# Residual-trunk kernel: in the down projections, one DMA-made sum is made by VectorE, and two operand sums are asked for later

## The chip, the cores and the metric

The kernel runs on 1 core of one Trainium2 chip. The time is the device time of one execution in microseconds (us); of several executions the median is taken. The engines are named as in the profile: PE (TensorE matmul), PEld (its weight loads), DVE (VectorE), ACT (ScalarE), POOL (GpSimd), SP (SyncE, which issues plain loads).

## What is computed

Two layers of a decoder trunk over 512 tokens of 1024 features, in float32. Each layer has four sub-layers: a SwiGLU feed-forward network, a token mixer, a cross-attention to 256 memory tokens, and a second SwiGLU network. The change lies in the feed-forward networks alone, of which there are four (two per layer):

```python
def swiglu_ffn(h, w_gu, w_down):      # w_gu (1024, 5632), w_down (2816, 1024)
    gu = h @ w_gu
    gate, up = jnp.split(gu, 2, axis=-1)
    return (jax.nn.silu(gate) * up) @ w_down

for i in range(DEPTH):                # DEPTH = 2
    f = swiglu_ffn(rms_norm(h, ffn1_pre_g[i]), ffn1_w_gu[i], ffn1_w_down[i])
    h = h + 0.5 * rms_norm(f, ffn1_post_g[i])
    ...                               # mixer and cross-attention
    f = swiglu_ffn(rms_norm(h, ffn2_pre_g[i]), ffn2_w_gu[i], ffn2_w_down[i])
    h = h + 0.5 * rms_norm(f, ffn2_post_g[i])
```

## The kernel before

**Split numbers.** Every float32 matrix is split into a high part (`whi` for weights, the first half of a `big` tile for operands), a cast by ACT (line 74), and a low part (`wlo`, or the second half of `big`), a subtraction by DVE (line 75). A product of two such numbers is three matmuls: lines 79 (high by high), 80 (high by weight low), 81 (operand low by weight high).

**The feed-forward network.** The 2816 hidden features are worked through in three groups, `FF_PARTS`. In each group the gate and up projections come first (`fm_quad`, then `seven` once per pair of 128 features, on the raw weights of line 242), then the down projection of that group. The first two groups hold 1024 features each, and their down projection is `seven_tm`, which is called eight times in the program: four times for a first group (here *first part*; its results are copied into the sums) and four times for a second group (*second part*; its results are added to them). The third group has a routine of its own.

**`seven_tm`** multiplies a 2 by 2 block matrix of hidden values (r11, r12, r21, r22) with a 2 by 2 block matrix of weights in seven block products in place of eight. The factors are sums of blocks: on the operand side x1 = r21 - r22, x2, x3 = r11 - r21 (line 414) and x4 (line 417), all by DVE; on the weight side T1 and T3. A block of weights is two tiles `raw`, called halves here, of 128 by 1024 numbers (512 KB) each. The products run on PE in this order: b11, T1 with x1, T1 (plus b22) with x2, b21 with r12, **T3 with x3**, b22 with x4, T1 (now with b21) with r22. Each product is 24 matmuls, 12 for each half of its weights.

**Sums of weights.** `load` (line 347) brings a block from HBM through SP; `put` (line 352) sends a second block from HBM onto the same tile with the DMA's own adder (`accum_op`), issued by POOL, which waits for the plain load to land first. T3 is block (0, 1) by `load` plus block (1, 1) by `put`. Block (1, 1) lies in the kernel's memory too, as b22, since its own product needs it. DVE already adds b22 to T1 (line 404).

**What sets the order.** The instructions of each engine run in a fixed order which a scheduler of the language lays down when the program is built; it starts from the order of the code and moves an instruction ahead of another where its model has it ready sooner. Each engine waits at the head of its own list for semaphores. Buffers limit how far ahead an engine may run: seven `raw` tiles, four `whi` and four `wlo` tiles. A `raw` tile is free for the next load once DVE has made its low part; a `whi` tile is free once PE has done the last of its 12 matmuls.

**Names.** The tiles carry numbers in the order of the built program. In the first call, `raw_1290` and `raw_1292` are the two halves of T3, `raw_1162` and `raw_1164` those of b22, `raw_1152` and `raw_1154` those of T1, `raw_1166` and `raw_1168` those of b21; in the second call (a second part) the same are `raw_2490`, `raw_2492`; `raw_2364`, `raw_2366`; `raw_2354`, `raw_2356`; `raw_2368`, `raw_2370`. Lines 387, 389 and 391 (in `take`) bring a product's result out of PSUM.

Of the kernel before, what the change touches and what calls it, by code (L numbers as in the profile page):

```python
# [8 lines left out]
ALU = mybir.AluOpType  # L9
# [26 lines left out]
def trunk_kernel(tc, x, mem, ffn1_pre_g, ffn1_w_gu, ffn1_w_down, ffn1_post_g,  # L36
# [7 lines left out]
    nc = tc.nc  # L44
    with ExitStack() as es:
# [290 lines left out]
        def seven_tm(w, k0, r, a11, f, fresh):  # L336
# [13 lines left out]
            def put(raws, kh, ch):  # L350
                for kk in range(2):
                    nc.gpsimd.dma_start(out=raws[kk], in_=rows(kh, kk, ch), accum_op=ALU.add)  # L352
# [16 lines left out]
            def product(n, raws, ops):  # L369
                start = n not in banks  # L370
                if start:
                    banks[n] = [psa(), psa()]
                for kk in range(2):
                    wh = parts(raws[kk], (P, 2, 512))
                    for s_ in range(2):
                        for i in range(2):
                            k = 2 * kk + i
                            cs = slice(s_ * P, (s_ + 1) * P)
                            mm3(banks[n][s_], (ops[:, 0, k, cs], ops[:, 1, k, cs]), (wh[0][:, i], wh[1][:, i]),
                                start and k == 0, k == 3, False)  # L380
                return banks[n]

            def take(th, ch, ps, how):
                for s_ in range(2):
                    dst = f[th][:, s_, ch * 512:(ch + 1) * 512]
                    if how is None:
                        nc.scalar.copy(out=dst, in_=ps[s_])
                    elif how == "from":
                        nc.vector.tensor_tensor(out=dst, in0=ps[s_], in1=dst, op=sub)
                    else:  # L390
                        nc.vector.tensor_tensor(out=dst, in0=dst, in1=ps[s_], op=how)
# [16 lines left out]
            a12 = operand(r12)  # L408
            u2 = product("A", t1, x2)
            t3 = load(0, 1)  # L410
            put(t3, 1, 1)
            put(t1, 1, 0)
            take(0, 1, u2, None if fresh else "from")
            nc.vector.tensor_tensor(out=r11, in0=r11, in1=r21, op=sub)
            x3 = operand(r11)
            take(0, 0, product("B", b21, a12), add)
            nc.vector.tensor_tensor(out=e, in0=e, in1=r12, op=add)
            x4 = operand(e)
            take(1, 1, product("A", t3, x3), sub)
            a22 = operand(r22)  # L420
            take(0, 1, product("C", b22, x4), "from")
            take(1, 0, product("A", t1, a22), None if fresh else add)
# [552 lines left out]
        rows = qt([P, P])  # L975
# [64 lines left out]
```

## Time and profile before

| | us |
|---|---|
| median of 3 runs | 2033.12 (2029.88 to 2033.5) |
| the profiled execution, its own time | 2035.78 |
| its span, first to last instruction | 2034.1 |
| PE busy in the span | 1962.7 (96%) |
| DVE busy | 1488.5 (73%) |
| ACT busy | 1037.4 (51%) |
| mean granted clock of PE, share of full speed | 0.993 |

The span is 1.7 us shorter than the execution's own time. "Busy" is the time in which an engine has at least one instruction running; the matmuls of PE overlap one another and their ends are modelled, so two matmuls in a row that show no idle time between them can still start late. Where an exact figure is wanted, the starts of matmuls are compared. "DMA share" is the mean busy share of the core's 16 DMA engines.

### The profile page before, as it was taken

How to read it: one execution, taken by the hardware profiler on the slowest of the kernel's cores; microseconds unless marked ns; L12 is line 12 of the kernel's file. 1: busy time of each engine (PE TensorE's matmuls, PEld its weight loads, DVE VectorE, ACT ScalarE, POOL GpSimd, SP SyncE). 2: the span in 40 equal slices, each digit the busy share in tenths (PEclk: the TensorE clock that was granted, in tenths of full speed). 3: DMA queues.
4: the chain of work that ended last, by engine and by line, in shares of the span. 5: the costliest groups of instructions: out<-in, count | busy, mean ns of one | idle time of the engine just before them, and what ended most of it. 6: DMA issues, size and time to landing. Idle time of an engine off the chain costs nothing. (4 is left out here: it accounts for less than half of the span.)

```text
span 2034.1 us, 31756 instructions
## 1 busy us (share of the span) xinstructions
PE 1962.7 (96%) x12841; PEld 1788.2 (88%) x12841; DVE 1488.5 (73%) x1831; ACT 1037.4 (51%) x1477; POOL 234.0 (12%) x229
## 2 busy tenths in 40 slices
PE   7999999998999999999999999999999999999998
PEld 7979889888878879899898979989878879989797
DVE  6776877799956558777886877787666648776875
ACT  6555445543555355555454555445535545545452
POOL 1111110122011011110101111110000001111100
PEclk9999999999999999999999999999999999999999
DMA  6877685323642145787873668696152225787771
GB/s 198 217 166 198 161 212 155 110 89 124 225 148 94 52 114 139 172 202 181 191 214 73 169 156 204 169 215 197 53 186 73 83 52 145 184 200 198 172 189 44
DMA packets 245929, 311.51 MB, mean 153 GB/s; under 512 B 9500, under 2 KB 189300, under 8 KB 244758
## 3 DMA queue, kind: packets, MB, share of 16 engines
q1 hardware_dynamic: 189158, 233.93, 35.9%
q0 software_dynamic: 56448, 75.51, 21.9%
q8 instruction: 100, 1.64, 0.3%
q14 instruction: 47, 0.39, 0.1%
q10 hardware_dynamic: 176, 0.05, 0.0%
HBM read 303.15 MB, written 6.29 MB: 152 GB/s over the span
## 5 line engine op out<-in xcount | busy, mean ns | idle before, releaser
L79 PE MATMUL psa<-big,whi 128*128 128x256 f32 (+1 forms) x3056 | 885.2, 291 | 6.2 <-ACT big L74 4.5
L81 PE MATMUL psa<-big,wlo 128*128 128x256 f32 (+1 forms) x3056 | 885.4, 290 | 5.6 <-DVE wlo L75 5.6
L80 PE MATMUL psa<-big,whi 128*128 128x256 f32 (+1 forms) x3056 | 887.1, 291 | 0.8 <-DVE big L75 0.8
L74 ACT CAST whi<-raw 128x1024 fp32r<-128x1024 f32 x522 | 544.3, 1049 | 622.8 <-PE psa L80 275.4
L75 DVE TENSOR_TENSOR wlo<-raw,whi 128x1024 fp32r<-128x1024 f32 x522 | 635.6, 1225 | 283.1 <-ACT whi L74 280.6
L79 PEld LDWEIGHTS psa<-big,whi 128*128 128x128 f32 x3056 | 587.6, 193 | 16.7 <-ACT big L74 8.3
L81 PEld LDWEIGHTS psa<-big,wlo 128*128 128x128 f32 x3056 | 588.0, 193 | 13.6 <-DVE wlo L75 6.7
L80 PEld LDWEIGHTS psa<-big,whi 128*128 128x128 f32 x3056 | 588.7, 193 | 9.1 <-DVE big L75 1.8
L79 PE MATMUL psa<-whi,big 128*128 128x512 f32 x864 | 341.5, 397 | 19.2 <-ACT whi L74 11.5
L80 PE MATMUL psa<-wlo,big 128*128 128x512 f32 x864 | 340.4, 394 | 6.1 <-DVE wlo L75 6.1
L81 PE MATMUL psa<-whi,big 128*128 128x512 f32 x864 | 339.3, 395 | 0.5
L79 PEld LDWEIGHTS psa<-whi,big 128*128 128x128 f32 x864 | 162.9, 189 | 60.7 <-ACT whi L74 16.6
L80 PEld LDWEIGHTS psa<-wlo,big 128*128 128x128 f32 x864 | 164.0, 190 | 42.7 <-DVE wlo L75 9.7
L81 PEld LDWEIGHTS psa<-whi,big 128*128 128x128 f32 x864 | 163.8, 190 | 39.7 <-DVE big L75 5.8
L302 POOL DMA_DIRECT2D raw<-in_ffn_w_gu_dram x40 | 51.6, 1289 | 611.9 <-DMA raw<-in_ffn_w_gu_dram 419.2
L158 POOL TENSOR_TENSOR r<-m,nhalf 128x1 f32<-128x1 f32 x74 | 49.0, 662 | 461.0 <-DVE m L532 182.3
L352 POOL DMA_DIRECT2D raw<-in_ffn_w_down_dram x48 | 57.3, 1193 | 332.7 <-DMA raw<-in_ffn_w_down_dram 229.5
L729 DVE SCALAR_TENSOR_TENSOR big<-big,par 128x511 f32<-128x511 f32 (+29 forms) x120 | 85.7, 767 | 0.0
L79 PE MATMUL psa<-big 128*128 128x512 f32 (+1 forms) x224 | 80.9, 363 | 0.8 <-ACT big L74 0.8
L297 POOL DMA_DIRECT2D raw<-in_ffn_w_gu_dram x40 | 53.0, 1326 | 244.7 <-DMA raw<-in_ffn_w_gu_dram 223.4
L80 PE MATMUL psa<-big 128*128 128x512 f32 (+1 forms) x224 | 80.7, 360 | 0.0
L81 PE MATMUL psa<-big 128*128 128x512 f32 (+1 forms) x224 | 80.2, 359 | 0.0
(150 smaller groups left out, 1658.2 us busy)
## 6 DMA issues: line engine op xcount, KB each, us to landing
raw<-in_ffn_w_gu_dram SPq DMA_DIRECT2D x216, 512.0 KB, 4.8
raw<-in_ffn_w_down_dram SPq DMA_DIRECT2D x104, 512.0 KB, 4.0
raw<-in_ffn_w_gu_dram POOLq DMA_DIRECT2D x80, 512.0 KB, 7.8
raw<-in_ffn_w_down_dram POOLq DMA_DIRECT2D x48, 512.0 KB, 6.1
raw<-in_xa_w_kv_dram SPq DMA_DIRECT2D x32, 512.0 KB, 3.5
raw<-in_ev_w_in_dram SPq DMA_DIRECT2D x16, 512.0 KB, 4.3
raw<-in_xa_w_q_dram SPq DMA_DIRECT2D x16, 512.0 KB, 3.7
raw<-in_xa_w_o_dram SPq DMA_DIRECT2D x16, 512.0 KB, 3.9
```

Of the source, the lines that this page charges most:

```text
L74: nc.scalar.copy(out=hi, in_=src)
L75: nc.vector.tensor_tensor(out=lo, in0=src, in1=hi.bitcast(F32), op=ALU.subtract)
L79: nc.tensor.matmul(out=ps, lhsT=lhs[0], rhs=rhs[0], start=start, stop=skip, skip_group_check=skip)
L80: nc.tensor.matmul(out=ps, lhsT=lhs[0], rhs=rhs[1], start=False, stop=skip, skip_group_check=skip)
L81: nc.tensor.matmul(out=ps, lhsT=lhs[1], rhs=rhs[0], start=False, stop=stop or skip, skip_group_check=skip)
L158: nc.gpsimd.tensor_tensor(out=r, in0=m, in1=nhalf.broadcast_to([P, n]), op=ALU.pow)
L297: nc.gpsimd.dma_start(out=t1, in_=fm_rows(w, 0, ca), accum_op=ALU.add)
L302: nc.gpsimd.dma_start(out=t3, in_=fm_rows(w, 1, cb), accum_op=ALU.add)
L352: nc.gpsimd.dma_start(out=raws[kk], in_=rows(kh, kk, ch), accum_op=ALU.add)
L729: nc.vector.scalar_tensor_tensor(out=acc[:, c, s_:], in0=z[:, c, :SEQ - s_], scalar=par[:, c, CONV - 1 - s_:CONV - s_], in1=acc[:, c, s_:] ...
```

## The change

Only `seven_tm` is changed. The second half of T3 is no longer completed by the DMA's adder: its `put` is dropped, and DVE adds the second half of b22 to it (new line 417). The first half stays with the DMA's adder (new line 411). In the code the product of b21 now stands ahead of the sum for x3, and the product of T3 ahead of the sum for x4. Behind the new line the line numbers are one or two higher (the sum for x3 is line 415, that for x4 line 419).

```diff
--- before.py
+++ after.py
@@ -408,15 +408,16 @@
             a12 = operand(r12)
             u2 = product("A", t1, x2)
             t3 = load(0, 1)
-            put(t3, 1, 1)
+            nc.gpsimd.dma_start(out=t3[0], in_=rows(1, 0, 1), accum_op=ALU.add)
             put(t1, 1, 0)
             take(0, 1, u2, None if fresh else "from")
+            take(0, 0, product("B", b21, a12), add)
             nc.vector.tensor_tensor(out=r11, in0=r11, in1=r21, op=sub)
             x3 = operand(r11)
-            take(0, 0, product("B", b21, a12), add)
+            nc.vector.tensor_tensor(out=t3[1], in0=t3[1], in1=b22[1], op=add)
+            take(1, 1, product("A", t3, x3), sub)
             nc.vector.tensor_tensor(out=e, in0=e, in1=r12, op=add)
             x4 = operand(e)
-            take(1, 1, product("A", t3, x3), sub)
             a22 = operand(r22)
             take(0, 1, product("C", b22, x4), "from")
             take(1, 0, product("A", t1, a22), None if fresh else add)
```

DVE, first call, a first part: from the sum for x4 (line 417 before, 419 after) on. `wlo_1345` and `wlo_1361` are the low parts of T3's halves before, `wlo_1341` and `wlo_1357` after; `big_1301` and `big_1336` are x3. Before:

```order
L417 TENSOR_TENSOR q4_1170<-q4_1170,big_220 128x1024
L75 TENSOR_TENSOR big_1255<-big_220,big_1255 128x1024
L75 TENSOR_TENSOR wlo_1323<-raw_1168,whi_1322 128x1024
L75 TENSOR_TENSOR wlo_1345<-raw_1290,whi_1344 128x1024
L75 TENSOR_TENSOR big_1301<-big_219,big_1301 128x1024
L75 TENSOR_TENSOR wlo_1361<-raw_1292,whi_1360 128x1024
L391 TENSOR_TENSOR big_1209<-big_1209,psa_1304 128x512
L75 TENSOR_TENSOR big_1341<-q4_1170,big_1341 128x1024
L391 TENSOR_TENSOR big_1209<-big_1209,psa_1305 128x512
```

After:

```order
L419 TENSOR_TENSOR q4_1170<-q4_1170,big_220 128x1024
L75 TENSOR_TENSOR big_1255<-big_220,big_1255 128x1024
L75 TENSOR_TENSOR wlo_1318<-raw_1168,whi_1317 128x1024
L75 TENSOR_TENSOR wlo_1341<-raw_1290,whi_1340 128x1024
L417 TENSOR_TENSOR raw_1292<-raw_1292,raw_1164 128x1024
L75 TENSOR_TENSOR big_1336<-big_219,big_1336 128x1024
L75 TENSOR_TENSOR wlo_1357<-raw_1292,whi_1356 128x1024
L75 TENSOR_TENSOR wlo_1382<-raw_1162,whi_1381 128x1024
L391 TENSOR_TENSOR big_1209<-big_1209,psa_1299 128x512
L391 TENSOR_TENSOR big_1209<-big_1209,psa_1300 128x512
```

The sums for x3 (further up) and x4 stand where they stood; the new sum has come in between the low part of T3's first half and that of x3. The low part of T3's second half follows that of x3 as before, and the low part of b22's first half (`wlo_1382`) has moved ahead of the b21 product's results and of x4's low part.

DVE, second call, a second part, from the low part of r12 on. `wlo_2507` and `wlo_2523` are the halves of b21 before, `wlo_2502` and `wlo_2518` after; T3's halves are `wlo_2545` and `wlo_2561` before, `wlo_2541` and `wlo_2557` after. Before:

```order
L75 TENSOR_TENSOR big_2455<-big_1450,big_2455 128x1024
L414 TENSOR_TENSOR big_1449<-big_1449 128x4x256
L75 TENSOR_TENSOR wlo_2507<-raw_2368,whi_2506 128x1024
L389 TENSOR_TENSOR big_1209<-psa_2377,big_1209 128x512
L75 TENSOR_TENSOR wlo_2523<-raw_2370,whi_2522 128x1024
L389 TENSOR_TENSOR big_1209<-psa_2378,big_1209 128x512
L75 TENSOR_TENSOR big_2501<-big_1449,big_2501 128x1024
L417 TENSOR_TENSOR q4_2372<-q4_2372,big_1450 128x1024
L75 TENSOR_TENSOR wlo_2545<-raw_2490,whi_2544 128x1024
```

After:

```order
L75 TENSOR_TENSOR big_2455<-big_1450,big_2455 128x1024
L75 TENSOR_TENSOR wlo_2502<-raw_2368,whi_2501 128x1024
L75 TENSOR_TENSOR wlo_2518<-raw_2370,whi_2517 128x1024
L389 TENSOR_TENSOR big_1209<-psa_2377,big_1209 128x512
L415 TENSOR_TENSOR big_1449<-big_1449 128x4x256
L389 TENSOR_TENSOR big_1209<-psa_2378,big_1209 128x512
L417 TENSOR_TENSOR raw_2492<-raw_2492,raw_2366 128x1024
L75 TENSOR_TENSOR big_2536<-big_1449,big_2536 128x1024
L75 TENSOR_TENSOR wlo_2541<-raw_2490,whi_2540 128x1024
L391 TENSOR_TENSOR big_1209<-big_1209,psa_2499 128x512
L391 TENSOR_TENSOR big_1209<-big_1209,psa_2500 128x512
L75 TENSOR_TENSOR wlo_2557<-raw_2492,whi_2556 128x1024
```

Here both operand sums have moved back: the sum for x3 behind the halves of b21 and one result, the sum for x4 behind the low part of T3's second half; the new sum stands between the second of these results and the low part of x3.

POOL, first call: the transfers with the adder behind those of T1. Before:

```order
L352 DMA raw_1290<-in_ffn1_w_down_dram 128x2x512
L352 DMA raw_1152<-in_ffn1_w_down_dram 128x2x512
L352 DMA raw_1154<-in_ffn1_w_down_dram 128x2x512
L352 DMA raw_1292<-in_ffn1_w_down_dram 128x2x512
L297 DMA raw_1451<-in_ffn1_w_gu_dram 128x4x256
L302 DMA raw_1460<-in_ffn1_w_gu_dram 128x4x256
```

After:

```order
L411 DMA raw_1290<-in_ffn1_w_down_dram 128x2x512
L352 DMA raw_1152<-in_ffn1_w_down_dram 128x2x512
L352 DMA raw_1154<-in_ffn1_w_down_dram 128x2x512
L297 DMA raw_1451<-in_ffn1_w_gu_dram 128x4x256
L302 DMA raw_1460<-in_ffn1_w_gu_dram 128x4x256
```

The transfer onto `raw_1292` is gone; what stood behind it has moved up by one. On SP the loads stand in the same order in both kernels, and on PE the seven products do.

## Rows read from the trace of the kernel before

**Rows 1.** page, part 1: busy us (share of the span), instructions

```profile
PE 1962.7 (96%) x12841; PEld 1788.2 (88%) x12841; DVE 1488.5 (73%) x1831; ACT 1037.4 (51%) x1477; POOL 234.0 (12%) x229
```

**Rows 2.** timeline of PE, first part: start, us, instruction, [idle before <-its end]

```profile
131.96 0.50 PE L79 MATMUL psa<-whi,big 128*128 128x512 f32 x1 [0.94 <-ACT whi L74]
133.22 0.50 PE L80 MATMUL psa<-wlo,big 128*128 128x512 f32 x1 [0.76 <-DVE wlo L75]
...
137.83 0.50 PE L80 MATMUL psa<-wlo,big 128*128 128x512 f32 x1 [1.55 <-DVE wlo L75]
```

**Rows 3.** timeline of PE, second part

```profile
257.05 0.73 PE L79 MATMUL psa<-whi,big 128*128 128x512 f32 x2 [1.41 <-ACT whi L74]
```

**Rows 4.** timeline of ACT: cast of T3's second half, first and second part

```profile
130.87 1.04 ACT L74 CAST whi<-raw 128x1024 fp32r<-128x1024 f32 x1 [6.43 <-DMA raw<-in_ffn_w_down_dram]
...
255.95 1.99 ACT L74 CAST whi<-raw 128x1024 fp32r<-128x1024 f32 x2 [1.94 <-DMA raw<-in_ffn_w_down_dram]
```

**Rows 5.** timeline of POOL: the adder's transfer for that half, two calls

```profile
122.73 1.20 POOL L352 DMA_DIRECT2D raw<-in_ffn_w_down_dram  x1 [6.31 <-DMA raw<-in_ffn_w_down_dram]
...
250.30 1.20 POOL L352 DMA_DIRECT2D raw<-in_ffn_w_down_dram  x1 [8.55 <-DMA raw<-in_ffn_w_down_dram]
```

**Rows 6.** timeline of SP: the plain load of the same half, two calls

```profile
118.37 0.37 SPq L347 DMA_DIRECT2D raw<-in_ffn_w_down_dram  x1
...
246.47 0.37 SPq L347 DMA_DIRECT2D raw<-in_ffn_w_down_dram  x1
```

**Rows 7.** windows, 72 matmuls from T3 on, first parts: length, PE busy, clock, DMA

```profile
128.14:148.61 20.47, 9.46 (x24) 1.00 0.79 195
...
sum 82.87, PE 39.29; mean PE 9.82
```

**Rows 8.** the same, second parts

```profile
252.75:272.89 20.14, 9.73 (x24) 0.92 0.97 232
...
sum 77.49, PE 37.93; mean PE 9.48
```

**Rows 9.** windows, product ahead of T3, 24 matmuls, eight calls, same columns

```profile
122.70:128.13 5.43, 3.11 (x8) 1.00 0.85 195
...
sum 43.44, PE 24.89; mean PE 3.11
```

**Rows 10.** windows of low clock: length, five engines busy, granted clock, DMA

```profile
258.50:261.90 3.40, 3.40 (x9) 2.62 (x9) 2.71 (x3) 1.34 (x2) 0.00 (x0) 0.50 1.15 245
...
1794.50:1797.90 3.40, 3.40 (x9) 2.62 (x9) 3.40 (x5) 2.91 (x4) 0.00 (x0) 0.50 0.52 159
```

**Rows 11.** timeline of DVE, first part

```profile
120.53 2.35 DVE L75 TENSOR_TENSOR wlo<-raw,whi 128x1024 fp32r<-128x1024 f32 x2
124.46 1.23 DVE L75 TENSOR_TENSOR big<-big 128x1024 fp32r<-128x1024 f32 x1 [1.58 <-ACT big L74]
```

**Rows 12.** timeline of DVE, second part

```profile
244.04 1.22 DVE L414 TENSOR_TENSOR big<-big 128x1024 f32<-128x1024 f32 x1
245.17 1.22 DVE L75 TENSOR_TENSOR wlo<-raw,whi 128x1024 fp32r<-128x1024 f32 x1
...
248.04 0.68 DVE L389 TENSOR_TENSOR big<-psa,big 128x512 f32<-128x512 f32 x1
...
252.95 0.69 DVE L391 TENSOR_TENSOR big<-big,psa 128x512 f32<-128x512 f32 x1 [0.22 <-PE psa L81]
```

**Rows 13.** groups by line: count | busy us, mean ns | idle before

```profile
L74 ACT CAST whi<-raw 128x1024 fp32r<-128x1024 f32 x522 | 544.3, 1049 | 622.8 <-PE psa L80 275.4 <-issue 145.3 <-PE psa L81 120.2
...
L404 DVE TENSOR_TENSOR raw<-raw 128x1024 f32<-128x1024 f32 x16 | 19.6, 1222 | 0.3
```

**Rows 14.** windows ahead of T3: length, PE, PEld, DVE (third), ACT, POOL busy

```profile
109.00:131.00 22.00, 21.18 (x91) 16.56 (x90) 15.08 (x14) 11.36 (x15) 4.86 (x4) 1.00 0.85 171
233.00:256.00 23.00, 21.80 (x93) 16.75 (x91) 22.53 (x24) 10.57 (x12) 4.86 (x4) 1.00 0.67 138
```

**Rows 15.** line 347, the 80 plain loads, issue to landing

```profile
DMA to landing us min/median/max: 3.2/3.9/5.6
```

## The prediction

> **What bounds the kernel now.** First the page: PE is busy for 96% of the span, DVE for 73% [rows 1]. PE's work is the same in both kernels, so the question is which stops of PE the change removes or makes. The timeline of PE, read for idle time behind the start of T3's product, shows them: in the first call 0.94, 0.76 and 1.55 us [rows 2], in the second (a second part) 1.41 us [rows 3]. All eight calls have such stops at that place. What they wait for stands in ACT's timeline: the cast of T3's second half starts at 130.87 after 6.43 us of idling for a DMA, in the second part at 255.95 [rows 4]. That DMA is the adder's transfer, which POOL issued at 122.73 and 250.30, as soon as the plain load of the same tile had landed [rows 5]; the load had been issued at 118.37 and 246.47 [rows 6]. So the half goes through two transfers in a row: 4.4 us for the load, then 8.1 us for the adder; 3.8 and 5.7 in the second part. ACT's later casts (b22, x4) queue behind the waiting one, and DVE's low parts behind them, hence the third stop of the first call, which is on b22.
>
> **What those stops cost.** Idle time alone does not tell, since matmuls overlap and the clock moves. So I compare lengths. A product without stops takes 43.44 / 8 = 5.43 us (24 matmuls; the rows count line 79 alone, a third of them) [rows 9]; three of them 16.3. From the first matmul on T3 to the end of the call there are three products, and they take 82.87 us over the four first parts and 77.49 over the four second parts [rows 7, 8]. Lost: 82.87 - 65.2 = 17.7 and 77.49 - 65.2 = 12.3, together 30.0 us, or 1.5% of the span. Of this, four calls have a stretch of 3.4 us right behind the stop (the first and the last of them are shown) in which the granted clock is 0.50, that is 1.2 GHz of 2.4, with nine matmuls in all where there would be about fifteen [rows 10]: half of 3.4 is 1.7 us each, 6.8 in all. The waits themselves are then 23.2.
>
> The clock rows show that a fall comes only behind a stop here, but also that four of the eight calls have stops and no fall. The Trainium skill, "Perfetto Trace Analysis", section "Matmul Optimizations", says that TensorE scales power with its utilization, so that matmuls should run back to back. By that rule the falls go with the stops and the ceiling of the gain is 30.0; if they came anyway, it would be 23.2. The trace has no fall within an unbroken run of products, which is for the first.
>
> **The change part by part.** *Removed:* eight transfers with the adder, one per call. On POOL that frees 1.2 us per call [rows 5], which nobody waits for. T3's second half is then ready one VectorE sum after its load, not one transfer after it.
>
> *Added:* eight sums on DVE. The same operation on the same shapes, line 404, takes 1.222 us, and line 74's cast 1.049 [rows 13]; in a row DVE instructions of this size start every 1.13 us [rows 12]. Eight times 1.13 is 9 us of DVE time, which lies beside PE's work if DVE has room, and that differs by part: ahead of T3 DVE is busy 15.08 of 22 us in a first part, but 22.53 of 23 in a second [rows 14].
>
> *First part, worked through on the first call.* The new sum stands behind the low part of T3's first half, which is done at 122.9 [rows 11]. The load has landed by 122.73, so DVE does not wait: sum until 124.1. The low part of x3 follows at 124.46 as before [rows 11] (its cast is the limit). The cast of T3's second half starts at about 124.4 instead of 130.87, its low part is done by 126.9. PE starts T3 at 128.14 and its second half 12 matmuls, or 2.7 us, later, at 130.9: four us of room. The casts for b22 wait only for PE to free a buffer then, and x4's low part, now behind b21's results, is done by about 130.4; PE needs it at 133.6. I take nothing lost: first parts gain all 17.7.
>
> *Second part, on the second call.* Here the sums that were moved matter. The low part of b21's first half, which frees the buffer for T3's second half, stood behind x3's sum and began at 245.17; it now begins at 244.04, where that sum was [rows 12]. The load goes out at 245.3 instead of 246.47, and by the same 3.8 us lands at 249.2. DVE gets to the new sum at 248.65 (it has the same work ahead of it as before 248.04 plus one result) [rows 12], waits 0.55, ends it at 250.4. Then x3's low part to 251.6 and that of T3's first half to 252.7; PE wants the latter at 252.98, its second matmul of T3. T3's second half: after b21's last result, which PE gives at 252.95 [rows 12], DVE makes the low part by 254.8; PE needs it at 255.5. From there it is tight: x4's sum, b22's first low part, a result of T3's product (not before 257.05), x4's low part until 259.0, another result, r22's low part, b22's second low part until 261.9. PE wants x4's low part at 259.1 (the order on PE puts four matmuls without it first) and the last at 261.8. I take 0.2 us lost per call, 0.8 in all, as the steps miss by 0.1 or less; second parts gain 12.3 - 0.8 = 11.5.
>
> *Bounds of the new wait.* No row shows DVE waiting for a plain load in front of such a sum. From below it costs nothing (the load has landed). From above I take the longest of the 80 loads of line 347, 5.6 us against a median of 3.9 [rows 15]: landing at 250.9, T3's first low part at 254.4, PE 1.4 us late in a second part, 5.6 us in all, and with a fall of the clock behind each another 6.8. In a first part even that load hides in the four us. The 0.2 is nearer the lower end because the four second-part loads are alike in kind and place, and the one shown takes 3.8.
>
> *What is late next.* The products behind `seven_tm` are `seven` of the next pair, on loads released by DVE's low parts. T3's second half and b22 are split six us earlier than before in a first part, so most of these loads go out earlier by more than PE does; b22's second half in a second part is split at 261.9, about as before, and the last load behind it is wanted only as fifth product. I cost this at nothing. The DMA engines lose eight transfers of 512 KB.
>
> **Sum.** 17.7 + 11.5 = 29.2 us. The profiled execution took 2035.78 (span 2034.1 and 1.7 around it); 2035.78 - 29.2 = 2006.6. The median of the runs shown is 2033.12, 2.7 below the profiled one; the same step below gives **2004**.
>
> **Rivals.**
> *A: DVE becomes the bound in second parts.* For it: 22.53 of 23 us busy, and 1.13 more put there [rows 14]; against it: the stretch behind is looser, and the order puts nothing else in. If PE waits there as long as today, only first parts gain: 2033.1 - 17.7 = 2015.4. The Trainium skill, "Perfetto Trace Analysis", section "Optimizing Scalar/DVE Operations", advises to move work off DVE when it is saturated, and this change moves work onto it; by that rule A is what happens, and the rows of second parts agree that DVE is full, those of first parts do not.
> *B: the gain is given back in the next products.* PE comes to them up to four us earlier and waits for their weights; the DMA share in the stretches shown is already 0.79 and 0.97 [rows 7, 8]. Against it: those loads hang on buffers freed by the same work that gets earlier. Given back whole, the time is 2033.
> *C: slower, by the queue of DVE.* Everything that DVE does waits behind the new sum until its load lands. It decides where the load lands after about 250 in a second part and 126 in a first, and each us beyond is a us of PE. To end 0.2% slower it has to eat the 29.2 and 4 more, 4.2 us per call: loads of over 8 us in second parts and 11 in first, against a longest of 5.6 [rows 15]. Time then: 2037 or more.
> *D: the change does not do what it says.* In first parts it half doesn't: the sums for x3 and x4 stand where they stood. There the removed transfer alone does the work, so no other time follows.
>
> **How the numbers follow.** The forecast gets 0.74 (1999 to 2011: it takes in the 5.6 above, and a clock fall more or less elsewhere), A and cases between 0.16 (2011 to 2018), B 0.06, C 0.04. The range 1998 to 2018 leaves out B and C and some tails. About 0.2% (4 us) is what a measurement of this kernel can tell from no change; faster by more than that 0.90, within it 0.06, slower 0.04.
>
> **What would show it.** In the changed kernel the stretches of 72 matmuls should be 16.3 to 16.7 us at a clock of 1.00; ACT should cast T3's second half near 124.4 after the first call's x3, with no DMA named ahead of it; the new line should idle DVE for under 1 us, in second parts alone. Stretches of 20 us in second parts only would be A; stops of PE on the weights of line 242, B; long idling of DVE ahead of line 417, C. The size of the gain is wrong if the low clock shows up at other stops instead.

## The result and the profile after

The changed kernel takes 2007.33 us in the median (2006.87 to 2010.79 over four runs; the kernel before beside it 2033.31), a ratio of 0.9875 with a 95% interval of 0.9854 to 0.9896. Another four runs, later on another occasion, gave 0.9882 (0.9865 to 0.9900). The change gains 1.2%, some 25 us. The profiled execution took 2006.9 us, its span is 2005.2.

The page's first part, which answers to [rows 1]:

```profile
PE 1950.1 (97%) x12841; PEld 1781.8 (89%) x12841; DVE 1496.5 (75%) x1839; ACT 1037.2 (52%) x1477; POOL 224.6 (11%) x221
```

DVE has 8 instructions and 8 us more, POOL 8 instructions and 9 us less; PE does the same matmuls.

The 72 matmuls from the start of T3 on, first parts, the same columns as [rows 7]: length, PE busy in line 79 alone, granted clock, DMA share, GB/s:

```profile
126.94:143.26 16.32, 9.34 (x24) 1.00 1.00 233
...
1766.26:1782.58 16.32, 9.34 (x24) 1.00 0.97 232
sum 65.26, PE 37.34; mean PE 9.34
```

The same for second parts, as [rows 8]:

```profile
247.41:263.94 16.53, 8.87 (x24) 1.00 0.88 230
970.35:987.36 17.01, 8.87 (x24) 1.00 0.84 223
1312.82:1329.35 16.53, 8.87 (x24) 1.00 0.86 231
1886.71:1903.24 16.53, 8.87 (x24) 1.00 0.86 228
sum 66.60, PE 35.49; mean PE 8.87
```

82.87 has become 65.26, and 77.49 has become 66.60: 17.6 + 10.9 = 28.5 us, of a difference of 28.9 between the two spans. Three products without stops take 16.3, so first parts lose nothing any more and second parts 1.4 us in all. The clock is 1.00 in all eight; the four falls behind the stops [rows 10] are gone with the stops. The rule that the prediction cites from the Trainium skill, "Perfetto Trace Analysis", section "Matmul Optimizations" (power scales with utilization, so matmuls should run back to back), agrees with these rows.

The rest is read from the stretches around the calls, over all lines of PE. First before (from b11 to T3 in the first call, from the end of that call to the second, from the end of the second to the third), then after:

```profile
104.93:128.14 23.21, 22.39 (x98) 1.00 0.69 137
...
148.61:229.25 80.64, 80.64 (x673) 1.00 0.80 199
...
272.89:835.15 562.26, 544.95 (x3433) 0.99 0.45 133
```

```profile
103.73:126.94 23.21, 22.39 (x98) 1.00 0.65 137
...
143.26:223.90 80.64, 80.64 (x674) 1.00 0.78 195
...
263.94:826.68 562.74, 543.91 (x3434) 0.99 0.45 133
```

The stretch behind a first part is 80.64 in both (in all four calls, within 0.01): nothing is given back in the next products. What is left of the 28.9 is 1.2 us by which the first call starts earlier (103.73 for 104.93), with up to 0.5 us lost in each of a few stretches far from the change, 0.8 in all. The 1.2 us need not come from the change: in five kernels with the adder on both halves of T3 (the kernel before and four of the experiments), which are alike up to there in a first part, T3 of the first call starts anywhere between 125.57 and 128.14, and in the changed kernel run again it starts at 127.63 for 126.94. No run here tells why.

### The profile page after: what moved, and what is told of

Same layout as the page of the kernel before. It is cut to its first block, busy times and chain, and to the rows that moved or that the text cites. A ratio compares the mean times of both kernels' runs of the same rounds, so it can differ in the third digit from the quotient of the medians.

```text
span 2005.2 us, 31747 instructions
## 1 busy us (share of the span) xinstructions
PE 1950.1 (97%) x12841; PEld 1781.8 (89%) x12841; DVE 1496.5 (75%) x1839; ACT 1037.2 (52%) x1477; POOL 224.6 (11%) x221
## 4 chain that ended last, share of the span: by engine, by line
PE 80%; DVE 8%; issue 5%; ACT 3%; POOL 2%; DMA 1%; POOLq 0%; ACTq 0%; SPq 0%; DVEq 0%
PE psa L81 26%; PE psa L80 26%; PE psa L79 26%; DVE wlo L75 2%; POOL r L158 1%; DVE big L75 1%; ACT q L175 1%; DVE big L730 1%; PE tps L182 1%; ACT whi L74 1%; DMA raw<-in_ffn_w_gu_dram 1%; ACT q L166 1%; DVE h L479 0%; DVE raw L404 0%; DVE q L394 0%
## 5 line engine op out<-in xcount | busy, mean ns | idle before, releaser
L79 PE MATMUL psa<-whi,big 128*128 128x512 f32 x864 | 337.2, 393 | 7.7 <-ACT big L74 6.2
L81 PE MATMUL psa<-whi,big 128*128 128x512 f32 x864 | 336.3, 392 | 0.5
L74 ACT CAST big<-big 128x512 fp32r<-128x512 f32 (+1 forms) x70 | 57.6, 827 | 31.9 <-DVE big L184 12.9
```

The costliest lines, as they stand in the source:

```text
L74: nc.scalar.copy(out=hi, in_=src)
L79: nc.tensor.matmul(out=ps, lhsT=lhs[0], rhs=rhs[0], start=start, stop=skip, skip_group_check=skip)
L81: nc.tensor.matmul(out=ps, lhsT=lhs[1], rhs=rhs[0], start=False, stop=stop or skip, skip_group_check=skip)
```

## What the engines do there now

ACT's timeline, first call, which answers to [rows 4]: the cast of x3 and, behind it, that of T3's second half:

```profile
122.19 1.05 ACT L74 CAST big<-big 128x1024 fp32r<-128x1024 f32 x1
123.13 1.05 ACT L74 CAST whi<-raw 128x1024 fp32r<-128x1024 f32 x1
```

No idle time stands in front of it, and no DMA. It begins 3.8 us ahead of T3's start at 126.94; before, it began at 130.87, 2.7 us behind it.

DVE's timeline, second call, around the new sum (line 417), and then the new sum of the fourth call:

```profile
242.71 0.68 DVE L389 TENSOR_TENSOR big<-psa,big 128x512 f32<-128x512 f32 x1
243.57 1.23 DVE L417 TENSOR_TENSOR raw<-raw 128x1024 f32<-128x1024 f32 x1 [0.18 <-DMA raw<-in_ffn_w_down_dram]
244.72 1.22 DVE L75 TENSOR_TENSOR big<-big 128x1024 fp32r<-128x1024 f32 x1
245.85 1.22 DVE L75 TENSOR_TENSOR wlo<-raw,whi 128x1024 fp32r<-128x1024 f32 x1
```

```profile
967.22 1.22 DVE L417 TENSOR_TENSOR raw<-raw 128x1024 f32<-128x1024 f32 x1 [0.87 <-DMA raw<-in_ffn_w_down_dram]
```

Line 417 as a whole, all eight calls (count, ns min/median/max; then how long DVE idled ahead of it, and how often):

```profile
L417 DVE TENSOR_TENSOR raw<-raw x8: 1215/1225/1228, 121.6 to 1883.0; 128x1024 f32<-128x1024 f32 x8
its engine sat idle before it (us, times) until:
  DMA raw<-in_ffn_w_down_dram: 1.8, 4
```

So the sum does wait for its load sometimes, 1.8 us in all. One of the four waits, 0.53 us in the fifth call, is in a first part; the stretch behind it is 16.31 all the same. The one stretch of 17.01 us is the call with the wait of 0.87.

## The experiments

All are of one core, timed beside the kernel before; the ratio is to that, with its 95% interval. "Lost" means the length of the 72 matmuls from T3 on, less 65.2 for four calls.

| kernel | median us | ratio | lost, first parts | lost, second parts |
|---|---|---|---|---|
| before | 2029.6 to 2034.5 | 1 | 17.7 | 12.3 |
| after | 2007.33 | 0.9875 (0.9854 to 0.9896) | 0.1 | 1.4 |
| the VectorE sum alone | 2010.87 | 0.9888 (0.9864 to 0.9913) | 0.0 | 5.3 |
| the order alone | 2044.03 | 1.0062 (1.0042 to 1.0081) | 17.5 | 24.7 |
| the sum three times | 2021.92 | 0.9952 (0.9929 to 0.9976) | 0.4 | 16.4 |
| both halves by VectorE | 2023.40 | 0.9952 (0.9930 to 0.9973) | 0.0 | 6.9 |
| the other half by VectorE | 2053.39 | 1.0111 (1.0088 to 1.0133) | 4.2 | 34.7 |
| order alone, b21 only | 2033.57 | 1.0009 (0.9994 to 1.0024) | 17.4 | 10.6 |
| order alone, T3 only | 2049.72 | 1.0097 (1.0075 to 1.0119) | 17.0 | 27.5 |
| T3 only, low part later | 2038.86 | 1.0020 (1.0009 to 1.0032) | 16.0 | 14.6 |
| sum on GpSimd | 2013.72 | 0.9904 (0.9887 to 0.9920) | 0.1 | 10.2 |
| b21 second | 2001.69 | 0.9855 (0.9837 to 0.9873) | 0.1 | 4.6 |
| b21 second, GpSimd in second parts | 2008.97 | 0.9883 (0.9868 to 0.9898) | 0.1 | 4.3 |
| after, again | 2008.60 | 0.9882 (0.9865 to 0.9900) | 0.1 | 1.5 |

### One part of the change at a time

The VectorE sum alone, with the sums for x3 and x4 asked for as in the kernel before (against the changed kernel):

```diff
-            take(0, 0, product("B", b21, a12), add)
             nc.vector.tensor_tensor(out=r11, in0=r11, in1=r21, op=sub)
             x3 = operand(r11)
+            take(0, 0, product("B", b21, a12), add)
             nc.vector.tensor_tensor(out=t3[1], in0=t3[1], in1=b22[1], op=add)
-            take(1, 1, product("A", t3, x3), sub)
             nc.vector.tensor_tensor(out=e, in0=e, in1=r12, op=add)
             x4 = operand(e)
+            take(1, 1, product("A", t3, x3), sub)
```

> VectorE sums the second half of T3, but the sums for x3 and x4 are asked for where they were asked for before. Theory (the adder's second transfer is the whole cause in first parts; in second parts the low part of T3's first half must also be early enough on VectorE): first parts lose nothing (72 matmuls from T3 on in 16.3 us each), in second parts the low part of b21 stays behind the sum for x3, the load goes out 1.1 us later than in the changed kernel, and T3's first low part, now behind the sum for x4 and two results, is ready about 2 us after PE wants it: 18.3 to 20 us per stretch, total about 2013 to 2019 us. Rival (the new sum alone does it, the moved sums do nothing): 16.3 to 16.7 us in second parts too, total 2007 us.

Windows of its second parts, columns as above:

```profile
246.13:263.75 17.62, 9.13 (x24) 1.00 0.82 217
...
sum 70.52, PE 36.53; mean PE 9.13
```

First parts are at 65.24, so there the sum alone does all of it. In second parts 77.49 - 70.52 = 7.0 us come from the sum and 70.52 - 66.60 = 3.9 from the order. The theory held, at a lower price than expected: a second part loses 1.3 us, where 2 to 3.7 were forecast, and the time is below the forecast. The times alone do not tell this kernel from the changed one (0.9888 and 0.9875, with intervals that overlap); the 3.9 us are read from the windows. DVE's timeline shows what the order buys: without it, the low part of T3's first half comes behind x4's sum and b21's results, at 246.94, 0.8 us behind T3's start at 246.13. In the changed kernel it starts at 245.85, 1.6 us ahead of T3's start.

```profile
244.31 1.22 DVE L418 TENSOR_TENSOR q<-q,big 128x1024 f32<-128x1024 f32 x1
245.44 0.68 DVE L391 TENSOR_TENSOR big<-big,psa 128x512 f32<-128x512 f32 x1
246.33 0.69 DVE L391 TENSOR_TENSOR big<-big,psa 128x512 f32<-128x512 f32 x1 [0.21 <-PE psa L81]
246.94 1.22 DVE L75 TENSOR_TENSOR wlo<-raw,whi 128x1024 fp32r<-128x1024 f32 x1
```

PE stops for a cast and then, in its weight loads, for that low part, which ends at 248.16. Without the first stop it would have waited for the low part all the same:

```profile
247.42 0.73 PE L79 MATMUL psa<-whi,big 128*128 128x512 f32 x2 [0.68 <-ACT big L74]
```

```profile
248.21 0.19 PEld L80 LDWEIGHTS psa<-wlo,big 128*128 128x128 f32 x1 [0.49 <-DVE wlo L75]
```

The order alone, with the DMA's adder on both halves as before (against the changed kernel):

```diff
-            nc.gpsimd.dma_start(out=t3[0], in_=rows(1, 0, 1), accum_op=ALU.add)
+            put(t3, 1, 1)
...
-            nc.vector.tensor_tensor(out=t3[1], in0=t3[1], in1=b22[1], op=add)
```

> The DMA's adder makes both halves of T3 as before; only the order is changed (x3 and x4 asked for one product later). Theory: first parts keep their loss (sum of the four stretches about 82 to 83 us), since nothing moves there; in second parts the load goes out 1.1 us earlier and the stop shrinks from 1.4 us by about that much, with PE then still waiting about 1 us for the low part; total about 2025 to 2029 us. Rival (the order is what freed PE): 2007 us. Rival (order does nothing): 2033 us.

The theory and both rivals missed: the order that is worth 3.9 us beside the VectorE sum makes the kernel 0.6% slower without it, and all of that lies in second parts (24.7 us lost for 12.3). Two kernels with one move each, against the kernel before, take it apart:

```diff
+            take(0, 0, product("B", b21, a12), add)
             nc.vector.tensor_tensor(out=r11, in0=r11, in1=r21, op=sub)
             x3 = operand(r11)
-            take(0, 0, product("B", b21, a12), add)
```

> The kernel before (the DMA's adder on both halves of T3) with one of the two moves of order alone: the product of b21 asked for ahead of the sum for x3. With both moves and no VectorE sum the time was 2044, and the four second parts lost some 24 us behind T3's start where the kernel before loses 12. Two theories for that. Transfer: the low parts of b21 come earlier on VectorE, so the loads behind go out earlier and the adder's transfer runs among more of them (8.2 us in the second call, against 5.6 before); then this kernel, which has that move, loses nearly as much, 5.5 to 6.4 us per second part, 2040 to 2045 us, and the adder's transfer takes 7 us or more. Queue: ACT's cast of T3's second half, which waits for that transfer, stands ahead of the casts of x4 and r22 in place of behind them; here it stands ahead of r22's alone, so the second parts lose 3 to 4.5 us each: 2031 to 2037 us.

```diff
+            take(1, 1, product("A", t3, x3), sub)
             nc.vector.tensor_tensor(out=e, in0=e, in1=r12, op=add)
             x4 = operand(e)
-            take(1, 1, product("A", t3, x3), sub)
```

> The kernel before with the other of the two moves alone: the product of T3 asked for ahead of the sum for x4. The low parts of b21 stand where they stood, so loads go out as before. Transfer theory: the adder's transfer takes 5.5 to 6 us as before and second parts lose 3 to 4 us: 2030 to 2035 us. Queue theory: ACT's cast of T3's second half stands ahead of that of r22 here too, so this kernel and the one with the other move alone come out alike, second parts losing 3 to 4.5 us each.

It is the other move. That of b21 changes nothing that can be measured (1.0009), that of T3 costs 1%. The queue theory falls, since ACT casts in the same order in both (x4, T3's second half, r22); the transfer theory keeps its mechanism but had the wrong move. Second call of the kernel with T3 moved: POOL issues the adder's transfer, SP a load of line 242, and ACT waits for the transfer:

```profile
249.19 1.20 POOL L352 DMA_DIRECT2D raw<-in_ffn_w_down_dram  x1 [8.58 <-DVE big L75]
```

```profile
249.94 0.37 SPq L242 DMA_DIRECT2D raw<-in_ffn_w_gu_dram  x1
```

```profile
257.28 1.04 ACT L74 CAST whi<-raw 128x1024 fp32r<-128x1024 f32 x1 [5.12 <-DMA raw<-in_ffn_w_down_dram]
```

The landing of this transfer, by line 352 in that microsecond:

```profile
DMA to landing us min/median/max: 8.1/8.1/8.1
```

In the kernel before the same transfer is issued at 250.30 [rows 5] and takes 5.6 us, and SP's load goes out at 252.20:

```profile
DMA to landing us min/median/max: 5.6/5.6/5.6
```

```profile
252.20 0.37 SPq L242 DMA_DIRECT2D raw<-in_ffn_w_gu_dram  x1
```

That load is released by the low part of T3's first half, which frees a `raw` tile; the move puts this low part ahead of x4's sum, and the load leaves 0.75 us behind the adder's transfer in place of 1.9. Over the second parts of before and of these three kernels it is always so: 5.5 to 5.7 us (eight transfers) where the load leaves 1.8 us or more behind, 7.6 to 8.8 us (seven of eight) where it leaves 0.5 to 0.8 us behind; the eighth, with the load 0.4 us ahead, takes 6.9. First parts of the kernel before, with that load 0.03 to 0.18 us behind, take 8.0 to 8.4 (three of the four; 7.0 where it is 1.5 ahead). To test it, VectorE gets one instruction more, which only makes that low part later, in second parts (against the kernel with T3 moved):

```diff
             x3 = operand(r11)
             take(0, 0, product("B", b21, a12), add)
+            if not fresh:
+                nc.vector.tensor_tensor(out=t3[0], in0=t3[0], in1=t3[0], op=ALU.max)
             take(1, 1, product("A", t3, x3), sub)
```

> The kernel before with the move of T3's product alone (2049.7 us), and in second parts one VectorE instruction more: T3's first half is overwritten by the maximum of itself and itself, which changes no number and only makes its low part later. Of the runs so far, the adder's transfer of T3's second half takes 5.5 to 5.7 us where the load behind it (line 242, released by the low part of T3's first half) goes out 1.8 us or more after it, and 7.6 to 8.8 us where that load goes out 0.5 to 0.8 us after it, as in second parts of the kernel with this move alone, which lose 6 to 7.6 us each. Theory: that load is what makes the transfer long. Here it goes out at least a VectorE instruction later, so the transfer should fall back to 5.5 to 5.8 us in second parts although VectorE does more; PE waits for the late low part instead, some 2 us, and the second parts lose 2 to 4.5 us each: 2032 to 2043 us. Rival: the transfer is long for another reason (the order on ACT, the move itself): it stays at 7.5 us or more, second parts lose 6 us or more, and the time is 2050 us or more.

The second call of this kernel, SP's load, and the landing of the adder's transfer issued at 249.57:

```profile
253.98 0.37 SPq L242 DMA_DIRECT2D raw<-in_ffn_w_gu_dram  x1
```

```profile
DMA to landing us min/median/max: 5.8/5.8/5.8
```

With the load 4.4 us behind, the transfer is back at 5.6 to 5.8 us in all four second parts, the loss there falls from 27.5 to 14.6 us, and the ratio from 1.0097 to 1.0020, although VectorE does more. What is left is mostly the late low part itself (PE idles 1.46 us for it, and 0.77 for that of the second half). So the theory holds for second parts: a plain load that starts 0.5 to 0.8 us behind the adder's transfer goes with 2 to 3 us more, and moving the load away takes them off. The changed kernel can take the order since no adder's transfer is left for that load to meet.

### How much room VectorE has

The sum made three times (added, subtracted, added):

```diff
             nc.vector.tensor_tensor(out=t3[1], in0=t3[1], in1=b22[1], op=add)
+            nc.vector.tensor_tensor(out=t3[1], in0=t3[1], in1=b22[1], op=sub)
+            nc.vector.tensor_tensor(out=t3[1], in0=t3[1], in1=b22[1], op=add)
```

> The changed kernel with the new VectorE sum made three times (added, taken off, added again), that is 2.3 us more VectorE time per call at the same place. Theory (second parts have no room on VectorE, first parts about four us): first parts stay at 16.3 to 16.7 us per stretch, second parts get about 3 us longer each because T3's first low part is late by that, with or without a fall of the clock of 1.7 us: total 2019 to 2026 us. Rival (VectorE has room in both): 2007 to 2009 us. Rival (no room in either): over 2030 us.

Its second parts, columns as in the windows above, and then the 19 us ahead of T3's start in the first call (a first part) with all five engines, as [rows 14]:

```profile
248.21:269.06 20.85, 9.29 (x24) 0.92 0.73 188
...
1898.08:1917.72 19.64, 9.02 (x24) 1.00 0.76 198
sum 81.58, PE 36.85; mean PE 9.21
```

```profile
109.00:128.00 19.00, 18.17 (x79) 14.39 (x79) 18.74 (x18) 13.14 (x16) 3.69 (x3) 1.00 0.69 153
```

2.3 us more of VectorE per call cost first parts 0.1 each and second parts 15.0 in all, 3.7 each, with two falls of the clock; PE's stop on the low part of T3's first half is 2.6 to 3.3 us long there. In the first part DVE is busy for 18.74 of 19 us and PE still loses nothing: it is not the busy share that tells whether there is room, but how far ahead of PE its results are. In second parts PE stops for longer than the 2.3 us that were added, so by these figures no room is left there: rival A had a real price, and the change stays just short of it. A kernel with one sum more was not run.

Both halves by VectorE, no adder:

```diff
-            nc.gpsimd.dma_start(out=t3[0], in_=rows(1, 0, 1), accum_op=ALU.add)
...
-            nc.vector.tensor_tensor(out=t3[1], in0=t3[1], in1=b22[1], op=add)
+            for kk in range(2):
+                nc.vector.tensor_tensor(out=t3[kk], in0=t3[kk], in1=b22[kk], op=add)
```

> The changed kernel with both halves of T3 summed by VectorE, no adder on T3 at all: eight more transfers gone, eight more sums of 1.13 us on VectorE. Theory: first parts unchanged at 16.3 us, second parts 0.3 to 1.2 us longer each for want of room on VectorE, total 2008 to 2012 us. Rival (DMA traffic limits, so that each transfer less helps): below 2005 us.

Slower than expected. Behind T3 first parts lose nothing, but the sum of the first half stands early in VectorE's list, ahead of the low part of x1, and PE stops there, in each first part:

```profile
112.69 0.50 PE L81 MATMUL psa<-whi,big 128*128 128x512 f32 x1 [1.13 <-DVE big L75]
```

From b11 to T3 a first part now takes 24.5 us or more for 23.2 (26.0 in the one with a fall of the clock), and second parts lose 6.9 behind T3.

The halves swapped, VectorE on the first and the adder on the second:

```diff
-            nc.gpsimd.dma_start(out=t3[0], in_=rows(1, 0, 1), accum_op=ALU.add)
+            nc.gpsimd.dma_start(out=t3[1], in_=rows(1, 1, 1), accum_op=ALU.add)
...
-            nc.vector.tensor_tensor(out=t3[1], in0=t3[1], in1=b22[1], op=add)
+            nc.vector.tensor_tensor(out=t3[0], in0=t3[0], in1=b22[0], op=add)
```

> The changed kernel with the halves swapped: VectorE sums the first half of T3 and the DMA's adder completes the second. As many transfers are dropped and as many VectorE sums added as in the change. Theory (the gain is that the late half no longer goes through two transfers in a row): the second half's adder is late again, so first parts lose about 4.4 us behind T3's start as before, second parts 4 to 6 as with the order moved and the adder kept, and the sum of the first half costs some more ahead of it: 2035 to 2055 us. Rival (what helps is eight transfers of 512 KB fewer, on whichever half): 2007 to 2015 us.

As many transfers and sums as in the change, and 1.1% slower than before. The stop on the late half stays: in each second part PE idles 3.7 to 4.5 us for the cast of T3's second half, which waits for the adder's transfer. ACT and PE in the second call:

```profile
256.70 1.04 ACT L74 CAST whi<-raw 128x1024 fp32r<-128x1024 f32 x1 [8.41 <-DMA raw<-in_ffn_w_down_dram]
```

```profile
257.79 0.79 PE L79 MATMUL psa<-whi,big 128*128 128x512 f32 x1 [3.85 <-ACT whi L74]
```

So eight transfers fewer do not bring the gain; it takes the late half's. What fewer transfers are worth alone is not shown, since this kernel has the moved order too, which costs 12.4 us in second parts where the adder completes the late half. Two things in it were not as expected: second parts lose 8.7 us each for 4 to 6, and three of the four first parts lose next to nothing behind T3, since they have lost 2.8 to 3 us ahead of it (26.0 for 23.2), on the low part of x1 as with both halves and by a fall of the clock (0.93 in these three stretches).

The sum on GpSimd:

```diff
-            nc.vector.tensor_tensor(out=t3[1], in0=t3[1], in1=b22[1], op=add)
+            nc.gpsimd.tensor_tensor(out=t3[1], in0=t3[1], in1=b22[1], op=add)
```

> The changed kernel with the new sum of T3's second half made by GpSimd in place of VectorE; the rest of the code is as in the change. No row here shows a GpSimd operation of 128 by 1024 numbers, so its length is measured by this run. Theory (from the kernel with the sum made three times: in first parts VectorE has room, in second parts each us more on it delays PE): first parts stay at nothing lost as long as the sum ends within some 4 us more than VectorE's 1.2; second parts lose the 0.15 to 0.6 us of the changed kernel less what 1.1 us of VectorE time is worth, so about nothing, if GpSimd needs under 3 us: 2004 to 2008 us, the same as the changed kernel or a little below. Rival: GpSimd is several times slower, or slows VectorE beside it, and T3's second half is late again: each us beyond 4 costs PE a us in all eight calls, 2012 us or more.

Line 417 there (ns min/median/max), then POOL and DVE in the second call:

```profile
L417 POOL TENSOR_TENSOR raw<-raw x8: 2529/2953/3302, 119.9 to 1892.1; 128x1024 f32<-128x1024 f32 x8
```

```profile
242.27 3.27 POOL L417 TENSOR_TENSOR raw<-raw 128x1024 f32<-128x1024 f32 x1 [7.10 <-DVE big L389]
```

```profile
243.21 3.41 DVE L75 TENSOR_TENSOR big<-big 128x1024 fp32r<-128x1024 f32 x1
246.66 1.23 DVE L75 TENSOR_TENSOR wlo<-raw,whi 128x1024 fp32r<-128x1024 f32 x1
```

GpSimd needs some 3 us for what VectorE does in 1.2, and VectorE is not even relieved: the low part of x3, which begins while GpSimd runs, takes 3.41 us and ends 1.1 us behind GpSimd's end at 245.54, as if it had begun only then. In the first call one that begins 0.67 us ahead of GpSimd's end takes 1.75 and ends 1.1 us behind it too; in the fourth, one that begins 0.17 us ahead of GpSimd's start takes its usual 1.22. The Trainium skill, "SBUF — State Buffer", section "SBUF: two separate sides", says that the two engines share a pair of ports, which one of them locks for a whole instruction while the other is blocked; these rows agree. Second parts lose 10.2 us for 1.4. First parts lose 0.1, as in the changed kernel, though GpSimd spends 2.85 us on the sum in the first call, where issuing the adder's transfer took it 1.20 in the kernel before [rows 5]: its freed time is not what helps them. The time is the rival's, but not its loss in all eight calls.

### Another order, perhaps faster

The product of b21 in second place, the operands x1 and x2 later (against the changed kernel):

```diff
-            x1 = operand(e)
+            a12 = operand(r12)
...
+            x1 = operand(e)
+            take(0, 0, product("B", b21, a12), add)
...
-            a12 = operand(r12)
...
-            take(0, 0, product("B", b21, a12), add)
```

> The changed kernel, with the product of b21 asked for second, right behind that of b11, and the operands x1 and x2 (which T1's products need) later; the same work. In the changed kernel every call still has a stop of 0.77 us ahead of T1's first product, on the cast of x1, and from b11 to T3 takes 23.2 us (first parts) and 23.5 us (second) where four unbroken products take 21.8. Theory: only x1's lateness makes that stop; with 5.4 us of other product ahead of it the stretch falls to about 21.8 and the eight calls give back 1.4 to 1.7 us each, some 12 us: 1994 to 1998 us, a ratio to the kernel before near 0.982. Rival, the slow case C of the prediction: in this order the new sum of T3's second half stands early in VectorE's list of a first part, ahead of the low part of x2; if it waits there for its load, VectorE idles ahead of that line, and PE stops on an operand: 2000 us or more in the sum, and the idling is seen in front of the line of the sum.

The stretches from b11 to T3, first parts and then second (sums over four calls; PE, PEld, DVE, ACT, POOL), of the changed kernel and then of this one:

```profile
sum 92.85, PE 89.50 PEld 71.50 DVE 90.68 ACT 67.17 POOL 19.53; mean PE 22.38 PEld 17.88 DVE 22.67 ACT 16.79 POOL 4.88
...
sum 94.03, PE 90.70 PEld 71.17 DVE 91.84 ACT 50.72 POOL 18.53; mean PE 22.67 PEld 17.79 DVE 22.96 ACT 12.68 POOL 4.63
```

```profile
sum 87.16, PE 87.16 PEld 72.11 DVE 86.52 ACT 56.34 POOL 19.54; mean PE 21.79 PEld 18.03 DVE 21.63 ACT 14.09 POOL 4.88
...
sum 89.03, PE 87.81 PEld 71.48 DVE 88.37 ACT 46.26 POOL 19.56; mean PE 21.95 PEld 17.87 DVE 22.09 ACT 11.57 POOL 4.89
```

The stop on x1 is gone: 5.7 + 5.0 us gained, near the 12 of the theory. But second parts lose 4.6 behind T3 for 1.4: PE stops there for 0.30 and 0.40 us, each time for a result of VectorE, which is busy for 88.37 of 89.03 us ahead of T3. 3.2 us are given back, and 2.4 more in stretches outside the calls. 5.1 us are left in the span, about half of what was expected. The sum stands early in VectorE's list in first parts, as the rival said, but does not wait: line 417 shows no idle time ahead of it. The ratio, 0.9855, lies below both of the changed kernel's (0.9875, 0.9882), but the intervals overlap: probably 0.2% faster, not settled.

The same with the sum on GpSimd in second parts:

```diff
-            nc.vector.tensor_tensor(out=t3[1], in0=t3[1], in1=b22[1], op=add)
+            (nc.vector if fresh else nc.gpsimd).tensor_tensor(out=t3[1], in0=t3[1], in1=b22[1], op=add)
```

> The kernel with the product of b21 in second place, which took 2001.7 us, with the new sum on GpSimd in the four second parts and on VectorE in the four first parts. In the second parts of that kernel VectorE runs from 224 to 262 us of the second call with hardly a gap, and PE loses 0.47 us ahead of T3 and 1.07 behind it in each, waiting for VectorE. Theory: VectorE is the bound there, so taking 1.13 us from it gives back most of it, 1 to 1.5 us in each of four calls: 1996 to 1999 us. Rival: GpSimd's sum takes so long that T3's second half is late: second parts lose 2 us or more behind T3's start, 2003 us or more.

The rival's time, not its reason (second parts lose 1.1 us each behind T3, for 2 or more): it loses for the reason seen above. A low part beside GpSimd's sum takes 3.43 us, and everything behind it on VectorE is late. PE's timeline, second call, shows two stops that every second part now has; the first is new, the second was 0.30:

```profile
241.08 0.50 PE L80 MATMUL psa<-wlo,big 128*128 128x512 f32 x1 [1.30 <-DVE wlo L75]
...
247.51 0.47 PE L79 MATMUL psa<-whi,big 128*128 128x512 f32 x1 [0.91 <-DVE big L389]
```

The measure beside these two was the changed kernel, unaltered:

> The changed kernel once more, unaltered, beside the two others on the same chip: 2005 to 2009 us, nothing lost behind T3 in first parts and 0.15 to 0.65 us in second parts. Both theories expect the same; it is the measure for the other two.

2008.60 us, 0.1 and 1.5 us lost: as in its first profile.

## Why the prediction was right

**The loss at T3.** 30.0 us were put down to the stops; 28.5 came back. Of these 24.6 come with the VectorE sum alone and 3.9 with the order beside it. The halves-swapped kernel, which removes as many transfers and keeps the stop, shows that it was the late half's two transfers in a row.

**First parts.** 17.7 forecast, 17.6 found; the cast of T3's second half was to start 19.5 us behind b11's start and starts 19.4 behind it (123.13 and 103.73). The sum alone does it; that the moved sums do nothing there (D) held: with the order alone, first parts lose 17.5.

**Second parts.** 0.8 us were to be left; 1.4 are. Three calls lose 0.2, as worked out, and one 0.7, where the sum waited 0.87 us for its load; its 17.01 us lie outside the 16.3 to 16.7 named as the sign. The steps on the second call stand: a wait of 0.55 us was worked out, 0.18 is seen. That the moved order is needed there was said for the load; it is worth 3.9 of the 10.9 us, and the other 7.0 come without it.

**The clock.** 6.8 of the 30.0 us were to come back with the stops. All eight stretches run at 1.00.

**The sum.** 2006.6 for the profiled execution, 2006.9 measured. The forecast of 2004 for the median is 3.3 low, and the step that missed is the last one: the profiled execution of before lay 2.7 us above its median, and I carried that over; the profiled execution of after lies on its median. Of the 49 runs of the kernel before that were timed beside the experiments, those with the lower granted clock are the longer ones (2025.85 us at a mean of 0.997, 2040.59 at 0.991), and the profiled one had 0.993. So the 2.7 us were probably low clock, which the 30.0 hold already: the forecast took them off twice. No run tests that. One part of the hit on the profiled execution is luck: 28.5 for 29.2, with 1.2 us at the start of the kernel and 0.8 lost in other stretches that I had not counted.

**Rivals.** A (VectorE bound in second parts) is the nearest: two sums more cost 15.0 us there. The rule of the Trainium skill, "Perfetto Trace Analysis", section "Optimizing Scalar/DVE Operations" (move work off a saturated VectorE), did not decide this change; by the runs, VectorE was full in second parts and the sum still paid. B fell: the next stretch is 80.64 us in both kernels. C fell: 1.8 us of waiting in all, 0.87 at most, though one wait of 0.53 us is in a first part, where none was forecast. The 5.6 us taken as the longest of 80 loads were a weaker bound than it looked: the trace has the landing of 40 of them.

**Not foreseen.** That the order by itself would make the kernel slower. The prediction counted it as help for the load alone, and asked of no transfer what else starts beside it.

## What to carry to other kernels

A tile that is filled by two transfers in a row is ready late twice: where the second operand lies on the chip already, let an engine that has results in hand ahead of need do the second step, and look for the room in how far ahead its results are, not in its busy share. A change of order must be priced with what it releases: here the same two moves were worth 3.9 us with the sum on VectorE and cost 12.4 us without it, by way of a load that one of them let go a microsecond closer to the adder's transfer. One part of a change can pay only beside the other, as the order does here, while the sum pays alone; time them apart as well as together.

## What the runs showed of the hardware

In second parts, a transfer of 512 KB with the DMA's adder takes 5.5 to 5.7 us when the next plain load leaves 1.8 us or more behind it, and 7.6 to 8.8 us when one leaves 0.5 to 0.8 us behind it. With that load moved to 4.3 us or more behind, the 2 to 3 us were gone (5.6 to 5.8, four of four). In first parts of the kernel with the halves swapped, three transfers with a load 0.8 to 1.1 us behind them lie between, at 6.0 to 7.6 us. Which part of the transfer is slowed is open.

A GpSimd sum of two tiles of 128 by 1024 float32 numbers took 2.5 to 3.3 us where VectorE takes 1.22. A VectorE subtraction of that size that began beside it ended 1.1 us behind it, and so took up to 3.4 us.
